# A hybrid conv/retention decoder block: values ahead of the previous head's projection, later norm sums, a regrouped last score block and a shared tail

## The chip, the core and the metric

The kernel runs on one core of one Trainium2 chip. The core has five engines that run side by side and meet only at semaphores: TensorE (PE, with its weight loads shown as PEld), VectorE (DVE), ScalarE (ACT), GpSimd (POOL) and SyncE (SP), which issues most of the DMAs. The metric is the device time of one execution in microseconds; lower is better.

## The reference, cut to what matters

One decoder layer over 512 tokens of width 1024, in float32:

```python
h = rms_norm(x, norm_mix_g)
glu_in, q, k, v, g, gate_logits = split(h @ w_in)
a   = glu_in[:C] * sigmoid(glu_in[C:])             # conv branch
a   = silu(layer_norm(causal_depthwise_conv31(a)))
y_a = a @ w_conv_proj + conv_proj_b
q, k = rotary(q) * dk**-0.5, rotary(k)             # 4 heads, dk 256, dv 512
r   = retention(q, k, v)                           # (q k^T * decay) v, causal
r   = (r - mean(r)) * rsqrt(var(r) + eps)          # per head
y_b = (silu(g) * r * ret_norm_g) @ w_ret_proj
x   = x + (sigmoid(gA) * y_a + sigmoid(gB) * y_b) @ w_out
u   = causal_depthwise_conv3(rms_norm(x, norm_ffn_g) @ w_up)
x   = x + (silu(u[:F]) * u[F:]) @ w_down
out = rms_norm(x, norm_final_g)
```

## The kernel before

Everything is held transposed: features on the 128 partitions, the 512 tokens along the free axis. Each float32 matrix product is made of three passes in the reduced format fp32r, high*high, high*low and low*high, so every activation and every weight is split into a high and a low part (ACT makes the high one, DVE the low one). `unit` makes one 128-feature block of output: for 8 k-tiles, three matmuls of 512 columns each, 24 in all, into one of the 8 PSUM banks. Weights come as one stream of half-megabyte pieces in the order of use (`load_half`, `split_half`: ACT line 130, DVE line 131), two pieces ahead.

The four heads run in a loop. Head h makes four GLU blocks (its two convolution channels' inputs), two blocks of q and two of k with their rotation (`rope`), then, from head 1 on, the projection of head h-1's result (`ret_proj`, 8 units of 12 matmuls), then the values (`values`, 96 matmuls into four banks at once, lines 509 to 511), the scores (`scores`, four key blocks j of 512, 384, 256 and 128 query columns), four gate units, and the product of scores and values (`inner`). The depthwise convolution of 31 taps runs on DVE (line 451) at low priority, between other work. After the heads come the gates, the two output projections, the FFN and the tail.

Norms need a sum over partitions and then a reciprocal root of it on all partitions. `stat` does it in stages that are spread over the units by a counter: `later(n, fn)` runs `fn` when `tick()` has been called n times, and `unit` calls `tick()` once. First DVE folds the squares (lines 275 and 277), then, `wait[0]` ticks later, one matmul sums them (line 281), DVE takes the diagonal out (lines 292 and 297), GpSimd raises it to the power -0.5 (line 245), and two DMAs by way of DRAM spread the row over the partitions into tile `rB` or `nB`; `use` is called `wait[1]` ticks after that. For the first norm the ticks come in `unit_quad`, which runs four GLU blocks together over 8 k-tiles (12 matmuls each): one tick after k-tile `QSUM` = 5, one after the last. For a head's norm the waits are (3, 2), its `use` being lines 603 and 209 on DVE. The convolution's layer norm (`conv_norm`) starts after head 3: at its fourth tick `centre` writes the mean into a tile `muB` (ACT line 467), which takes the slot of tag `nB` (one buffer, shared with the head norm's row), DVE subtracts it (line 470) and sums squares, and four ticks later comes the matmul of line 281 for the variance.

The Tile framework orders the instructions of each engine ahead of time: it simulates the kernel with its own costs and lets each engine take, of the instructions that are ready in that simulation, the one that stands first in the program (with the priorities given). On the chip each engine then runs its list strictly in that order.

The tail works on the two token halves (256 columns). `late_half` makes the last two blocks of the down projection for one half (lines 739 to 741), with callbacks between its matmuls; `finish` gives the stages of the final norm. `early` sums what is known before the last block (four small matmuls, line 229), `first` adds the last block's square (four more) and takes the root on GpSimd, `second` spreads the root over the partitions with four matmuls (line 260, `fB`) and multiplies the eight blocks by it on DVE (line 779), two blocks to a tile, each tile sent out by one DMA from SP (line 781).

Of the kernel before, what the change touches and what calls it, by code (L numbers as in the profile page):

```python
# [14 lines left out]
P = 128  # L15
S = 512
# [13 lines left out]
LOOK = 2  # L30
QSUM = 5
WARM = 9
# [17 lines left out]
def hybrid_block(  # L50
# [29 lines left out]
    def tmp():  # L80
        return t512("t", 8)

    def bank():
        return psp.tile([P, S], F32, tag="ps", name=nm("ps"))
# [11 lines left out]
    warm = sb.tile([P, NCH], F32, tag="tok", bufs=8, name="warm")  # L96
    for tag, bufs, dt in (("x", 8, F32), ("xg", 16, F32R), ("A", 16, F32R), ("C", 8, F32),
                          ("R", 8, F32R), ("G", 4, F32), ("ss", 2, F32), ("t", 8, F32),
                          ("rB", 1, F32), ("nB", 1, F32), ("dec", 1, F32)):
        first[tag] = sb.tile([P, S], dt, tag=tag, bufs=bufs, name=nm(tag))  # L100
    cosr = sb.tile([P, S], F32, tag="cosr", name="cosr")
# [20 lines left out]
    raws = {}  # L122

    def load_half(h):
        raw = wide("wraw", F32, HS, 3)
        nc.sync.dma_start(out=raw, in_=wst[h])
        raws[h] = raw
# [84 lines left out]
    def split_scaled(src, g, tag, bufs):  # L212
        h = t512(tag, bufs, F32R)
        l = t512(tag, bufs, F32R)
# [33 lines left out]
    def spread_ps(ps, r, chunks=range(NCH)):  # L248

        sl = slice(chunks[0], chunks[-1] + 1)  # L250
        rh = tok(F32R)
        rl = tok(F32R)
        nc.vector.tensor_copy(out=rh[:, sl], in_=r[:, sl])
        nc.vector.tensor_tensor(out=rl[:, sl], in0=r[:, sl], in1=f32(rh[:, sl]), op=ALU.subtract)

        def run():
            for c in chunks:
                dst = ps[:, c * P:(c + 1) * P]
                for i, x in enumerate((rh, rl)):
                    nc.tensor.matmul(dst, lhsT=x[:, c:c + 1].broadcast_to([P, P]), rhs=identr,  # L260
                                     start=i == 0, stop=i == 1)
            return ps

        return run
# [197 lines left out]
    def conv_norm():  # L462
        run = sums(csum[0])

        def centre():
            muB = t512("nB", 1)
            nc.scalar.mul(out=muB, in_=run(), mul=1.0 / D)
# [6 lines left out]
        def scale(rs, _):  # L474
            for i in range(KT):
# [3 lines left out]
                                     scale=pcol("conv_ln_g", i), bias=pcol("conv_ln_b", i))  # L479
                h = t512("A", 16, F32R)  # L480
                l = t512("C", 8, F32R)
# [7 lines left out]
    def rope(p1=None):  # L489
# [3 lines left out]
        for u, v, op in ((p1, p2, ALU.subtract), (p2, p1, ALU.add)):  # L493
# [4 lines left out]
            nc.vector.tensor_tensor(out=m1, in0=m1, in1=m2, op=op)  # L498
            res.append(split(m1, "A", 16))
        return res  # L500

    def values():
# [12 lines left out]
        for c in range(NCH):  # L515
# [5 lines left out]
            nc.vector.tensor_scalar(out=m, in0=s, scalar1=-1.0 / DV, scalar2=None, op0=ALU.mult)  # L521
            h = t512("A", 16, F32R)
            l = t512("A", 16, F32R)
            nc.scalar.activation(out=h, in_=t, func=AF.Identity, bias=m)
# [7 lines left out]
    def scores(q, k, dec):  # L532
        sc = wide("sc", F32R, 2 * SW, 1)
        sh, sl_ = sc[:, :SW], sc[:, SW:]
        for j in range(NCH):
# [3 lines left out]
            for d in range(2):  # L539
                (qh, ql), (kh, kl) = q[d], k[d]  # L540
                nc.tensor.matmul(ps[:, :n], lhsT=kh[:, js], rhs=qh[:, j * P:], start=d == 0,
# [5 lines left out]
            t = tmp()  # L547
            nc.vector.tensor_tensor(out=t[:, :n], in0=ps[:, :n], in1=dec[:, :n], op=ALU.mult)
            o = slice(SOFF[j], SOFF[j] + n)
# [43 lines left out]
    def ret_norm(h, banks, sg):  # L593
# [11 lines left out]

        stat(sq.acc, DV, EPS, use, (3, 2), "nB")
        return res
# [15 lines left out]
    for h in range(H):  # L623
# [27 lines left out]
    conv_norm()  # L651
    sigA = [gate(m, t512("A", 16)) for m in range(KT)]
    for mp in range(KT // 2):
# [98 lines left out]
    def finish(half):  # L752
# [7 lines left out]
        def early(sqs):  # L760
# [24 lines left out]
        return early, first, second  # L785

    a_sums, a_rsqrt, a_out = finish(0)
    sqs = late_half(0, {(LATE - 1, HF - 2): a_sums})
    b_sums, b_rsqrt, b_out = finish(1)
    sqs = late_half(1, {(0, 4): lambda _: a_rsqrt(sqs), (1, 1): a_out, (LATE - 1, HF - 2): b_sums})  # L790
    b_rsqrt(sqs)
    b_out(None)
    assert pos[0] == 8 * NBLK
# [102 lines left out]
```

## Time and profile before

| | before |
|---|---|
| median of 3 runs | 1075.55 us (1075.36 to 1075.80) |
| profiled execution, its own time | 1075.43 us |
| span of the profiled execution | 1073.3 us |
| PE busy | 1058.7 us, 99% |
| DVE busy | 780.5 us, 73% |
| ACT busy | 429.7 us, 40% |
| mean granted TensorE clock | 0.996 |

The span runs from the first to the last instruction; 2.1 us of the execution's time lie outside it. A time of an instruction in a timeline is its start from the begin of the span. Matmuls overlap in the pipeline, so their durations are longer than the distance from one start to the next, and that distance is what counts.

### The profile page before, as it was taken

The numbers are of one execution on the slowest core, as the hardware profiler recorded it, in microseconds if no ns is written. First come the engines' busy times: TensorE is split into PE (matmuls) and PEld (weight loads), VectorE is DVE, ScalarE is ACT, GpSimd is POOL, SyncE is SP. The second block draws the span as 40 slices with busy tenths as digits, with TensorE's granted clock in tenths as the row PEclk, the third lists the DMA queues.
The fourth block names the chain that finished last, engine by engine and source line by source line (L and its number), as shares of the span: only waits on it lengthen the run. The fifth ranks groups of instructions, "written<-read, shape, count | busy, mean of one in ns | idle before, by whom it ended". The sixth has DMA issues, their size and how long they took to land.

```text
span 1073.3 us, 12462 instructions
## 1 busy us (share of the span) xinstructions
PE 1058.7 (99%) x4810; PEld 883.5 (82%) x4810; DVE 780.5 (73%) x1173; ACT 429.7 (40%) x577; POOL 26.1 (2%) x88
## 2 busy tenths in 40 slices
PE   9999999999999999999899999999999999999996
PEld 7888788888888888888788888888888888888886
DVE  7799989958997899957765555587776336777433
ACT  6343433543334431544552333354444113444331
POOL 0100100000000000000000000000000000000000
PEclk9999999999999999999999999999999999999999
DMA  8322232223223222223223442233222222222312
GB/s 286 100 97 90 62 105 94 93 80 98 101 95 99 71 96 99 82 78 106 89 99 99 146 128 98 91 105 110 98 98 93 98 93 92 96 99 98 98 59 79
DMA packets 34122, 107.32 MB, mean 100 GB/s; under 512 B 4048, under 2 KB 6992, under 8 KB 34064
## 3 DMA queue, kind: packets, MB, share of 16 engines
q1 hardware_dynamic: 32848, 104.42, 29.4%
q0 software_dynamic: 784, 1.85, 0.7%
q8 instruction: 37, 0.61, 0.2%
q10 hardware_dynamic: 432, 0.27, 0.1%
q14 instruction: 21, 0.17, 0.1%
HBM read 104.41 MB, written 2.11 MB: 99 GB/s over the span
## 4 chain that ended last, share of the span: by engine, by line
PE 84%; DVE 10%; DMA 2%; issue 2%; ACT 1%; POOL 0%; SPq 0%; POOLq 0%; DVEq 0%
PE ps L179 25%; PE ps L181 25%; PE ps L180 25%; DVE C L451 3%; PE ps L510 2%; PE ps L511 2%; PE ps L509 2%; DVE wlo L131 2%; PE ps L572 1%; DVE ss L221 1%; PE ps L574 1%; DMA G<-in_wst_dram 1%; DVE t L421 0%; DMA nB<-row 0%; DMA rB<-row 0%
## 5 line engine op out<-in xcount | busy, mean ns | idle before, releaser
L130 ACT CAST whi<-wraw 128x1024 fp32r<-128x1024 f32 (+2 forms) x184 | 191.5, 1041 | 319.6 <-PE ps L180 214.5
L131 DVE TENSOR_TENSOR wlo<-wraw,whi 128x1024 fp32r<-128x1024 f32 (+2 forms) x185 | 222.5, 1203 | 62.4 <-ACT whi L130 61.0
L181 PE MATMUL ps<-xg,wlo 128*128 128x512 f32 x656 | 256.0, 390 | 0.0
L179 PE MATMUL ps<-xg,whi 128*128 128x512 f32 x656 | 256.0, 390 | 0.0
L180 PE MATMUL ps<-xg,whi 128*128 128x512 f32 x656 | 256.0, 390 | 0.0
L181 PE MATMUL ps<-A,wlo 128*128 128x512 f32 x448 | 174.3, 389 | 0.0
L179 PE MATMUL ps<-A,whi 128*128 128x512 f32 x448 | 174.3, 389 | 0.0
L451 DVE SCALAR_TENSOR_TENSOR C<-ap,par,C 128x512 f32<-128x512 f32 x240 | 166.8, 740 | 2.3 <-ACT C L448 1.9
L180 PE MATMUL ps<-A,whi 128*128 128x512 f32 x384 | 149.4, 389 | 0.0
L181 PEld LDWEIGHTS ps<-xg,wlo 128*128 128x128 f32 x656 | 123.5, 188 | 25.8
L180 PEld LDWEIGHTS ps<-xg,whi 128*128 128x128 f32 x656 | 123.5, 188 | 25.6
L179 PEld LDWEIGHTS ps<-xg,whi 128*128 128x128 f32 x656 | 123.6, 188 | 25.3
L181 PEld LDWEIGHTS ps<-A,wlo 128*128 128x128 f32 x448 | 84.1, 188 | 17.5
L179 PEld LDWEIGHTS ps<-A,whi 128*128 128x128 f32 x448 | 84.1, 188 | 17.5
L180 PEld LDWEIGHTS ps<-A,whi 128*128 128x128 f32 x384 | 72.1, 188 | 14.9
L693 DVE SCALAR_TENSOR_TENSOR t<-ap,par,t 128x512 f32<-128x512 f32 x96 | 71.4, 748 | 1.7 <-issue 0.2
L221 DVE TENSOR_TENSOR x<-x,ps 128x512 f32<-128x512 f32 (+1 forms) x50 | 33.1, 661 | 52.6 <-PE ps L181 49.1
L687 DVE TENSOR_TENSOR ap<-ps,rB 128x512 f32<-128x512 f32 x48 | 32.8, 687 | 40.9 <-PE ps L181 37.7
L179 PE MATMUL ps<-R,whi 128*128 128x512 f32 x160 | 62.2, 389 | 0.0
L180 PE MATMUL ps<-R,whi 128*128 128x512 f32 x160 | 62.2, 389 | 0.0
L181 PE MATMUL ps<-R,wlo 128*128 128x512 f32 x160 | 62.2, 389 | 0.0
L421 DVE TENSOR_TENSOR t<-ps,rB 128x512 f32<-128x512 f32 x48 | 32.5, 684 | 33.9 <-PE ps L181 33.8
(154 smaller groups left out, 1204.8 us busy)
## 6 DMA issues: line engine op xcount, KB each, us to landing
wraw<-in_wst_dram SPq DMA_DIRECT2D x180, 512.0 KB, 3.3
x<-in_xT_dram SPq DMA_DIRECT2D x16, 256.0 KB, 3.3
out_dram<-t SPq DMA_DIRECT2D x8, 256.0 KB, 2.1
nB<-row POOLq DMA_DIRECT2D x5, 256.0 KB, 4.5
dec<-in_decay_dram SPq DMA_DIRECT2D x4, 256.0 KB, 2.6
wraw<-in_wst_dram SPq DMA_DIRECT2D x3, 256.0 KB, 5.3
G<-in_wst_dram SPq DMA_DIRECT2D x2, 256.0 KB, 5.7
t<-in_cs_dram SPq DMA_DIRECT2D x2, 256.0 KB, 3.9
```

Source lines behind the costliest of these rows:

```text
L130: (eng or nc.scalar.copy)(out=hi[:, sl], in_=raw[:, sl])
L131: nc.vector.tensor_tensor(out=lo[:, sl], in0=raw[:, sl], in1=f32(hi[:, sl]), op=ALU.subtract)
L179: nc.tensor.matmul(ps, lhsT=wh, rhs=xh, start=kt == 0, stop=False)
L180: nc.tensor.matmul(ps, lhsT=wh, rhs=xl, start=False, stop=False)
L181: nc.tensor.matmul(ps, lhsT=wl, rhs=xh, start=False, stop=kt == last)
L221: nc.vector.tensor_tensor(out=acc, in0=acc, in1=v, op=ALU.add)
L421: nc.vector.tensor_tensor(out=t, in0=ps, in1=rB[0], op=ALU.mult)
L451: nc.vector.scalar_tensor_tensor(out=acc, in0=a[:, k:k + S], scalar=wcol(k), in1=acc, op0=ALU.mult, op1=ALU.add)
L509: nc.tensor.matmul(banks[c], lhsT=xh[:, sl], rhs=wh, start=kt == 0, stop=False)
L510: nc.tensor.matmul(banks[c], lhsT=xl[:, sl], rhs=wh, start=False, stop=False)
L687: nc.vector.tensor_tensor(out=u[:, FK - 1:], in0=ps, in1=rB[0], op=ALU.mult)
L693: nc.vector.scalar_tensor_tensor(out=c, in0=u[:, k:k + S], scalar=wcol(k), in1=c, op0=ALU.mult, op1=ALU.add)
```

## The change

Five edits. Head h's values come before head h-1's projection, and the loads follow that order (`use_order`). The ticks of the norms move: `QSUM` from 5 to 6, the heads' waits from (3, 2) to (4, 3), and `muB` takes the slot of tag `dec` in place of `nB`. Of the score block j = 3 (128 query columns), the two products that share the weights `kh` become one matmul over 256 columns, high and low part of q side by side; ACT copies and DVE adds the two halves of the result afterwards. For that the high and the low part of a split lie in one tile of tag `A` (8 tiles of 1024 columns in place of 16 of 512). In the tail, half 0 makes its sum once (`whole`) in place of `early` and `first`, its callbacks come one k-tile later, and of half 1 the products of blocks 6 and 7 go to GpSimd, from a copy of the root that ACT takes out of a second spread, and out by a DMA from ACT; six matmuls whose results nobody reads are put between the tail's steps (`idle_work`).

```diff
-QSUM = 5
+QSUM = 6
...
+    def pair_a():
+
+        t = wide("A", F32R, 2 * S, 8)
+        return t[:, :S], t[:, S:], t.rearrange("p (i t) -> p i t", i=2)
...
+    use_order = list(range(NBLK))
+    for h in range(1, H):
+        b = 20 * h + 4
+        use_order[b:b + 8] = use_order[b + 4:b + 8] + use_order[b:b + 4]
+
     def load_half(h):
         raw = wide("wraw", F32, HS, 3)
-        nc.sync.dma_start(out=raw, in_=wst[h])
+        nc.sync.dma_start(out=raw, in_=wst[use_order[h]])
...
         def centre():
-            muB = t512("nB", 1)
+            muB = t512("dec", 1)
...
-                (qh, ql), (kh, kl) = q[d], k[d]
+                (qh, ql, qb), (kh, kl, _) = q[d], k[d]
+                if j == NCH - 1:
+                    for low in ((False, True) if d == 0 else (True, False)):
+                        if low:
+                            nc.tensor.matmul(ps[:, :n], lhsT=kl[:, js], rhs=qh[:, j * P:],
+                                             start=False, stop=False)
+                        else:
+                            nc.tensor.matmul(ps[:, :2 * n].rearrange("p (i t) -> p i t", i=2),
+                                             lhsT=kh[:, js], rhs=qb[:, :, j * P:],
+                                             start=d == 0, stop=d == 1)
+                    continue
...
+            if j == NCH - 1:
+                src = tmp()
+                nc.scalar.copy(out=src[:, :n], in_=ps[:, n:2 * n])
+                nc.vector.tensor_tensor(out=src[:, :n], in0=ps[:, :n], in1=src[:, :n], op=ALU.add)
+            nc.vector.tensor_tensor(out=t[:, :n], in0=src[:, :n], in1=dec[:, :n], op=ALU.mult)
...
-        stat(sq.acc, DV, EPS, use, (3, 2), "nB")
+        stat(sq.acc, DV, EPS, use, (4, 3), "nB")
...
         k = rope()
+        v = values()
         if rg is not None:
             ret_proj(h - 1, rg)
-        v = values()
...
+        def whole(sqs):
+            for q in sqs:
+                add_into(ss.acc[:, tk], q[:, :HT])
+            tok_sums(ps, [(ss.acc, 0)], chunks)
+            run.append(spread_ps(ps, rsqrt(scaled(ps, D, EPS, sl), sl), chunks))
...
         def second(_):
-            fB = run[0]()
-            for m in range(0, KT, 2):
+            fB = run[0]()[:, tk]
+            if half:
+                fS = tmp()[:, :HT]
+                nc.scalar.copy(out=fS, in_=run[0](bank())[:, tk])
+            for m in (KT - 2, *range(0, KT - 2, 2)) if half else range(0, KT, 2):
                 o = tmp()
+                aside = half and m == KT - 2
+                eng = nc.gpsimd if aside else nc.vector
                 for i in range(2):
-                    nc.vector.tensor_tensor(out=o[:, i * HT:(i + 1) * HT], in0=fB[:, tk],
-                                            in1=x1[m + i][:, tk], op=ALU.mult)
-                nc.sync.dma_start(
+                    eng.tensor_tensor(out=o[:, i * HT:(i + 1) * HT], in0=fS if aside else fB,
+                                      in1=x1[m + i][:, tk], op=ALU.mult)
+                (nc.scalar if aside else nc.sync).dma_start(
...
+    def idle_work(ps, n):
+
+        for _ in range(n):
+            nc.tensor.matmul(ps, lhsT=onesr, rhs=ff[HF][0], start=True, stop=True)
+
+    _, _, a_rsqrt, a_out = finish(0)
+    sqs = late_half(0, {})
+    b_sums, b_rsqrt, _, b_out = finish(1)
+    sqs = late_half(1, {(0, 5): lambda _: a_rsqrt(sqs), (1, 2): a_out, (LATE - 1, HF - 2): b_sums})
+    spare = bank()
+    idle_work(spare, 2)
     b_rsqrt(sqs)
+    idle_work(spare, 4)
     b_out(None)
```

## Rows read from the trace of the kernel before

**Rows 1.** Waits: engine, line, releaser; us in total, times, longest us.
```profile
PE ps L281 <- DVE t L277: 5.5, 3, 3.2
...
PE ps L260 <- DVE tokr L253: 1.2, 1, 1.2
...
PE ps L229 <- ACT t L747: 1.0, 1, 1.0
```
**Rows 2.** Timeline of PE: start us, us, what, [idle before].
```profile
23.60 0.61 PE L196 MATMUL ps<-xg,R 128*128 128x512 f32 x2
24.77 0.47 PE L281 MATMUL ps<-t,onesr 128*128 128x512 f32 x1 [0.56 <-DVE t L277]
...
121.17 0.39 PE L181 MATMUL ps<-xg,wlo 128*128 128x512 f32 x1
123.34 0.47 PE L281 MATMUL ps<-t,onesr 128*128 128x512 f32 x1 [1.78 <-DVE t L277]
...
511.23 0.39 PE L181 MATMUL ps<-xg,wlo 128*128 128x512 f32 x1
514.82 0.50 PE L281 MATMUL ps<-t,onesr 128*128 128x512 f32 x1 [3.20 <-DVE t L277]
...
518.77 0.42 PE L179 MATMUL ps<-xg,whi 128*128 128x512 f32 x1
```
**Rows 3.** Windows: stretch, its us, busy us of each engine, PEclk, DMA share, GB/s.
```profile
36.00:121.00 85.00, 85.00 (x396) 71.49 (x395) 84.97 (x135) 33.84 (x50) 0.24 (x2) 1.00 0.26 84
...
515.00:519.00 4.00, 4.00 (x11) 3.16 (x12) 3.96 (x10) 2.98 (x5) 0.00 (x0) 0.57 0.13 39
...
1069.00:1072.00 3.00, 0.00 (x0) 0.00 (x0) 1.22 (x4) 0.00 (x0) 0.00 (x0) 0.50 0.99 350
```
**Rows 4.** Timelines of DVE and ACT from 487 to 515 us.
```profile
487.00 0.17 DVE L297 TENSOR_SCALAR tok<-tok 128x4 f32<-128x4 f32 x1
...
495.29 1.90 DVE L603 TENSOR_TENSOR G<-G,nB 128x512 f32<-128x512 f32 x3 [3.49 <-DMA nB<-row]
...
498.42 0.60 ACT L467 ACTIVATE nB<-ps 128x512 f32<-128x512 f32 x1 [0.23 <-DVE G L603]
...
500.05 2.49 DVE L470 TENSOR_TENSOR C<-C,nB 128x512 f32<-128x512 f32 x4
...
514.08 0.69 DVE L277 TENSOR_TENSOR t<-t,t 64x512 fp32r<-64x512 f32 x1
```
**Rows 5.** DVE's instructions by line from 500 to 514.8 us; count, busy us, mean ns.
```profile
L209 DVE TENSOR_TENSOR R<-G,R 128x512 fp32r<-128x512 f32 x2 | 1.4, 676 | 0.0
```
**Rows 6.** Timeline of PE at head 0's last score block.
```profile
75.25 0.28 PE L545 MATMUL ps<-A,A 128*128 128x256 f32 x1
75.37 0.22 PE L541 MATMUL ps<-A,A 128*128 128x128 f32 x1
...
76.27 0.39 PE L180 MATMUL ps<-xg,whi 128*128 128x512 f32 x1
76.50 0.39 PE L181 MATMUL ps<-xg,wlo 128*128 128x512 f32 x1
```
**Rows 7.** Timelines of PE and DVE in the tail.
```profile
1052.86 0.28 PE L741 MATMUL ps<-xg,wlo 128*128 128x256 f32 x1
...
1053.55 0.28 PE L740 MATMUL ps<-xg,whi 128*128 128x256 f32 x1
...
1067.48 2.74 DVE L779 TENSOR_TENSOR t<-ps,x 128x256 f32<-128x256 f32 x8 [0.64 <-PE ps L260]
```
**Rows 8.** Timeline of POOL, its two copies of 128 columns.
```profile
1.08 0.29 POOL L390 CAST onesr<-ones 128x128 fp32r<-128x128 f32 x1
...
16.42 0.61 POOL L389 CAST identr<-ident 128x128 fp32r<-128x128 f32 x1 [15.05 <-DMA ident<-in_ident_dram]
```
**Rows 9.** Timeline of DVE in head 1.
```profile
130.35 0.68 DVE L421 TENSOR_TENSOR t<-ps,rB 128x512 f32<-128x512 f32 x1
...
137.60 1.89 DVE L603 TENSOR_TENSOR G<-G,nB 128x512 f32<-128x512 f32 x3 [4.18 <-DMA nB<-row]
```

More of the change, by code (lines that the diff above doesn't have):

```diff
@@ L81, in tmp, with half_a @@
         return t512("t", 8)
+    spare = {}
+    def pair_a():
+        t = wide("A", F32R, 2 * S, 8)
+        return t[:, :S], t[:, S:], t.rearrange("p (i t) -> p i t", i=2)
+    def half_a(dt=F32R):
+        if dt not in spare:
+            t = wide("A", dt, 2 * S, 8)
+            spare[dt] = t[:, S:]
+            return t[:, :S]
+        return spare.pop(dt)
     def bank():
@@ L96, in hybrid_block @@
     warm = sb.tile([P, NCH], F32, tag="tok", bufs=8, name="warm")
-    for tag, bufs, dt in (("x", 8, F32), ("xg", 16, F32R), ("A", 16, F32R), ("C", 8, F32),
+    for tag, bufs, dt in (("x", 8, F32), ("xg", 16, F32R), ("A", 8, F32R), ("C", 8, F32),
                           ("R", 8, F32R), ("G", 4, F32), ("ss", 2, F32), ("t", 8, F32),
                           ("rB", 1, F32), ("nB", 1, F32), ("dec", 1, F32)):
-        first[tag] = sb.tile([P, S], dt, tag=tag, bufs=bufs, name=nm(tag))
+        w = 2 * S if tag == "A" else S
+        first[tag] = sb.tile([P, w], dt, tag=tag, bufs=bufs, name=nm(tag))
     cosr = sb.tile([P, S], F32, tag="cosr", name="cosr")
@@ L212, in split_scaled @@
     def split_scaled(src, g, tag, bufs):
-        h = t512(tag, bufs, F32R)
-        l = t512(tag, bufs, F32R)
+        if tag == "A":
+            h, l, _ = pair_a()
+        else:
+            h = t512(tag, bufs, F32R)
+            l = t512(tag, bufs, F32R)
         nc.scalar.activation(out=h, in_=src, func=AF.Copy, scale=g)
@@ L254, in spread_ps, with run @@
         nc.vector.tensor_tensor(out=rl[:, sl], in0=r[:, sl], in1=f32(rh[:, sl]), op=ALU.subtract)
-        def run():
+        def run(dst=ps):
             for c in chunks:
-                dst = ps[:, c * P:(c + 1) * P]
                 for i, x in enumerate((rh, rl)):
-                    nc.tensor.matmul(dst, lhsT=x[:, c:c + 1].broadcast_to([P, P]), rhs=identr,
-                                     start=i == 0, stop=i == 1)
-            return ps
+                    nc.tensor.matmul(dst[:, c * P:(c + 1) * P], rhs=identr, start=i == 0,
+                                     lhsT=x[:, c:c + 1].broadcast_to([P, P]), stop=i == 1)
+            return dst
         return run
@@ L479, in scale @@
                                      scale=pcol("conv_ln_g", i), bias=pcol("conv_ln_b", i))
-                h = t512("A", 16, F32R)
+                h = half_a()
                 l = t512("C", 8, F32R)
@@ L498, in rope @@
             nc.vector.tensor_tensor(out=m1, in0=m1, in1=m2, op=op)
-            res.append(split(m1, "A", 16))
+            h, l, both = pair_a()
+            nc.scalar.copy(out=h, in_=m1)
+            nc.vector.tensor_tensor(out=l, in0=m1, in1=f32(h), op=ALU.subtract)
+            res.append((h, l, both))
         return res
@@ L521, in values @@
             nc.vector.tensor_scalar(out=m, in0=s, scalar1=-1.0 / DV, scalar2=None, op0=ALU.mult)
-            h = t512("A", 16, F32R)
-            l = t512("A", 16, F32R)
+            h, l, _ = pair_a()
             nc.scalar.activation(out=h, in_=t, func=AF.Identity, bias=m)
@@ L539, in scores @@
             for d in range(2):
-                (qh, ql), (kh, kl) = q[d], k[d]
+                (qh, ql, qb), (kh, kl, _) = q[d], k[d]
[4 more added lines that the diff above has]
+                                             start=False, stop=False)
+                        else:
+                            nc.tensor.matmul(ps[:, :2 * n].rearrange("p (i t) -> p i t", i=2),
+                                             lhsT=kh[:, js], rhs=qb[:, :, j * P:],
+                                             start=d == 0, stop=d == 1)
+                    continue
                 nc.tensor.matmul(ps[:, :n], lhsT=kh[:, js], rhs=qh[:, j * P:], start=d == 0,
@@ L547, in scores @@
             t = tmp()
-            nc.vector.tensor_tensor(out=t[:, :n], in0=ps[:, :n], in1=dec[:, :n], op=ALU.mult)
+            src = ps
+            if j == NCH - 1:
[3 more added lines that the diff above has]
+            nc.vector.tensor_tensor(out=t[:, :n], in0=src[:, :n], in1=dec[:, :n], op=ALU.mult)
             o = slice(SOFF[j], SOFF[j] + n)
@@ L651, in hybrid_block @@
     conv_norm()
-    sigA = [gate(m, t512("A", 16)) for m in range(KT)]
+    sigA = [gate(m, half_a(F32)) for m in range(KT)]
     for mp in range(KT // 2):
@@ L774, in second @@
         def second(_):
-            fB = run[0]()
-            for m in range(0, KT, 2):
+            fB = run[0]()[:, tk]
[3 more added lines that the diff above has]
+            for m in (KT - 2, *range(0, KT - 2, 2)) if half else range(0, KT, 2):
                 o = tmp()
+                aside = half and m == KT - 2
+                eng = nc.gpsimd if aside else nc.vector
                 for i in range(2):
-                    nc.vector.tensor_tensor(out=o[:, i * HT:(i + 1) * HT], in0=fB[:, tk],
-                                            in1=x1[m + i][:, tk], op=ALU.mult)
-                nc.sync.dma_start(
+                    eng.tensor_tensor(out=o[:, i * HT:(i + 1) * HT], in0=fS if aside else fB,
+                                      in1=x1[m + i][:, tk], op=ALU.mult)
+                (nc.scalar if aside else nc.sync).dma_start(
                     out=out[m * P:(m + 2) * P, tk].rearrange("(i p) t -> p i t", p=P),
                     in_=o.rearrange("p (i t) -> p i t", i=2))
[L785 to L790, printed above, removed]
+        return early, first, whole, second
+    def idle_work(ps, n):
[7 more added lines that the diff above has]
+    idle_work(spare, 2)
     b_rsqrt(sqs)
+    idle_work(spare, 4)
     b_out(None)
```

## The prediction

> **What bounds the kernel now.** I read the page first. PE is busy 99% of the span, DVE, the next, 73% (the table above), and for nearly the whole span PE starts one 512-column matmul every 0.227 us (0.23 in the two decimals of [rows 6], 76.27 to 76.50). So a time is saved in only two ways: less PE work, or fewer moments in which PE waits. A full list of PE's waits is short, which is why the next view is the one by waits [rows 1]: the matmul of line 281, the partition sum of a norm, waited for DVE 5.5 us in three places, the spread of the root (line 260) 1.2 us once, the tail's sum (line 229) 1.0 us once. Then the timeline of PE at those three places [rows 2] gives each its price as the distance between starts, less the 0.227 that it would be anyhow:
>
> - first norm: two matmuls from 23.60, so the next was due at 24.05; it started at 24.77: **0.72 us**.
> - head 0's norm: 121.17 to 123.34, less 0.227: **1.94 us**.
> - the convolution's layer norm: 511.23 to 514.82, less 0.227: 3.36 us. After it the clock is not whole: over 515 to 519 us the granted clock was 0.57 of 2.4 GHz [rows 3], so mostly at its lower level, 1.2 GHz. From 514.82 to 518.77 PE started ten matmuls in 3.95 us where 2.27 would do: 1.68 us more. Together **5.04 us**. The 1.94 us wait of head 0 was followed by no such loss.
>
> The last stretch is another regime. From 1069 to 1072 us the 16 DMA engines were busy 0.99 of the time and moved 350 GB/s, 1.05 MB, which is just the second half of the output (four tiles of 256 KB) [rows 3]. There the transfer sets the end, not DVE.
>
> **The change part by part.** Each sum is against the profiled execution, 1075.43 us (its span of 1073.3 and 2.1 outside it); the median of the runs is 0.12 higher.
>
> *QSUM 6.* The matmul of line 281 comes one k-tile later: 12 x 0.227 = 2.72 us, by when its input is long there. The 0.72 goes. In exchange the root arrives 2.72 - 0.72 = 2.0 us later, and with it everything that DVE does with it in head 0. PE does not need it at once: the banks that hold unscaled products are given back by DVE, and in the kernel before PE ran on over this whole stretch without a wait. Cost nothing on PE; DVE is 2.0 us later, which the next part must carry.
>
> *Head waits (4, 3).* Line 281 comes after the fourth unit, not the third: 24 x 0.227 = 5.45 us later. At head 0, where PE was due at 121.40, it is due at 126.85, less 0.95 because QSUM and the score block (below) bring PE there earlier: 125.9. DVE: it was busy 84.97 of the 85 us from 36 to 121 [rows 3], so nothing absorbs the later root, and its line 277 that let PE go at 123.34 comes at up to 123.34 + 2.0 + 0.3 (one more short addition for the score block; a 512-column operation is 1.90 / 3 = 0.63 [rows 4], a quarter of the columns at most half of that) = 125.6. It fits by 0.3 us. The planner may put one weight split more before it (1024 columns, so about 2 x 0.63 = 1.3 us): 1.0 us would remain. But the filler on DVE there is the low-priority convolution, which gives way, so I take 0 and keep 0 to 1.0. The 1.94 goes.
>
> *muB in `dec`.* Head 3's norm and the layer norm share the slot `nB`. ACT could write the mean only when line 603 had read the row (498.42, released by L603), DVE began line 470 at 500.05, and line 277 ended at 514.77, 14.7 us later, when PE had stood for 3.4 us [rows 4]. DVE itself waited 3.49 us for the row's DMA before line 603, with line 470 behind it in the order. With `dec`, which is free after head 3's scores, the mean needs only its own sum, four units of 24 before the matmul of 511.46 (due), so at 511.46 - 21.8 = 489.7. Head 3's own sum now stands in the same tick and just before it; its picking on DVE (four operations of 128 columns, at most half of 0.63 each, and line 297's 0.17) takes 1.4, a weight split 1.3: line 470 at about 492.5, line 277 done at 492.5 + 14.7 = 507.2, 4.3 us before PE asks. What could eat that: lines 603 and 209 of head 3 now fall in between, eight operations x 0.63 = 5.0 us, of which the 14.7 already hold two [rows 5], so 3.8; and the planner believes in the row sooner than it comes, so DVE can stand before line 603 again, up to the 3.49 of before. Worst: 507.2 + 3.8 + 3.5 = 514.5, a wait of 3.0 us. All three have lower rank in the program than the layer norm's chain, so they get only its gaps. I take 0, keep 0 to 3.0. The 5.04 goes, and the clock's 1.68 with it.
>
> *Values ahead of the projection.* The same matmuls and loads in another order; the swap is made in `use_order` too, and SP passes as many bytes. The head norm's row, 5.45 us later by its wait, is wanted 96 x 0.227 = 21.8 us later. Scores come after the projection, so the values' eviction on ACT has more time than before. Nothing; what it could cost is the rival that ends on the other side.
>
> *Score block j = 3.* Six 128-column matmuls: 75.37 to 76.27 less the one unit matmul's 0.227 = 0.67 us, 0.11 each though 256 columns take only 0.12 (75.25 to 75.37) [rows 6]: a matmul of 128 columns pays for its weights, not for its columns. Now two of 256 and two of 128: at 0.12 and 0.11 each 0.46, saving 0.21 to (if a short one next to a long one hides its weights) 0.27 a head. The strided pair of q could run slower than a plain 256; the bound there is no gain at all. I take 0.22 x 4 = **0.9 us**, keep 0 to 1.1. ACT's copy and DVE's addition lie under the four gate units (21.8 us) between scores and `inner`.
>
> *Pairs in `A`.* As many bytes in the same order of use: nothing; a pair's slot comes free with the later of its halves, and both were read by the same unit.
>
> *Tail, sums.* Half 0's separate early sum goes: 1052.86 to 1053.55 holds two matmuls of 256 (0.24) and the four small ones [rows 7]: 0.69 - 0.24 = **0.45 us** of PE. The callbacks one k-tile later give DVE time for its two additions.
>
> *Tail, products.* By DVE alone the last tile would be ready two products earlier, 2 x 2.74 / 8 = 0.69 us [rows 7]. But the transfer is the limit [rows 3]: it starts when the first tile is there, which is no earlier, and four tiles still have to pass. So I take 0. The Trainium skill says the same of the second queue (DMA: Bandwidth & Descriptors, Issuing engines are not separate DMA queues: DMAs started by different engines run on the same 16 DMA engines); before, no DMA was issued from ACT in the tail, so no row shows it, and without that rule the sum would be 0.69 lower. GpSimd may be late: the nearest rows are copies of 128 columns at 0.29 and 0.61 [rows 8], so 256 columns 0.58 to 1.22, two 1.2 to 2.4 us. They start about 1.05 us after DVE's first product (a second spread, four matmuls x 0.11, and ACT's copy, at most the 0.60 of its 512 columns in [rows 4]), so end 2.2 to 3.5 after it. The transfer starts 1069 - 1067.48 = 1.5 after that product, 0.8 after the first tile; three tiles take three quarters of 3 us, to 3.75, so the fourth must be ready by 2.95. Late by 0 to 0.55. The Trainium skill is against such work (GPSIMD Engine Reference, Elementwise — side-by-side cycle accounting: a two-input addition took 1.96 times VectorE's time); by it two products would take 2 x 2 x 0.34 = 1.4 us, which is inside the bounds and would leave the sum as it is.
>
> *Idle matmuls.* Two (0.45) in PE's wait of 1.0, four (0.91) in its wait of 1.2 [rows 1]: nothing; without that cover at most 0.3.
>
> Sum: 0.72 + 1.94 + 5.04 + 0.9 + 0.45 = 9.05. 1075.43 - 9.05 = 1066.38, so **1066.4 us**.
>
> **The rivals.**
>
> - *One wait comes back in part.* DVE is late at head 0 (0 to 1.0), at the layer norm (0 to 3.0), or GpSimd at the end (0 to 0.55): up to 4.6, 1067.4 to 1071.0. For it: DVE saturated to 121, the planner's optimism in all heads. Against: the margin of 4.3 us at the layer norm.
> - *The layer norm's wait stays whole,* because the planner puts line 603 before line 470 after all: 5.04 back, 1071.4 us. For it: that is today's order. Against: it was forced by the shared slot.
> - *Slower: values find no banks.* `values` needs four banks at once, right behind `rope`; the projection needed one every 2.7 us. Today DVE evicts the fourth GLU block at 130.35 and stands 4.18 us before line 603 at 137.60 [rows 9]; with the later wait that stop moves to about 143, in front of q's and k's rotations. If it also stood before a GLU eviction, more than four of eight banks were held when values start (150.9) and PE waited. It decides against the change from 9.05 / 3 = 3.0 us a head on; a wait like the layer norm's (3.36 + 1.68) in three heads gives 1066.4 + 15.1 = 1081.5. Against: the evictions lie 20 us before, and head 0 already runs in this order, without a wait.
> - *The change does not do it:* the waits move behind one another (DVE's work is the same), within 2 us of before.
>
> **How the numbers follow.** Likeliest (1065.4 to 1067.4): 0.6. One wait in part: 0.23. Layer norm's wait whole: 0.08. No change: 0.05. Slower: 0.04. The range goes down by the score block's best case (0.2) and by a transfer that gains the 0.69 after all, to 1065.4; and up to the end of the second case, 1071.0; it leaves out 0.17. A measurement here tells about 0.2%, 2.15 us, from nothing: faster 0.91, same 0.05, slower 0.04.
>
> **What would show it.** Line 281 without idle time before it near 26.8, 126 and 511 (less the shift), and a granted clock of 1.00 throughout; line 470 before or between lines 603, eight us earlier; 0.45 us for the four matmuls of block 3; one group of four line-229 matmuls less; DMA share 0.99 for 3 us at the end as before, with DVE's last product 0.7 us earlier relative to its first. Wrong, if PE shows a wait at line 509 in heads 1 to 3, a wait of over 2 us at line 281, or an end that comes after GpSimd's tile.

## The result and the profile after

The changed kernel took 1067.01 us (median of 6 runs, 1066.19 to 1067.72), the kernel before, beside it on the same chip, 1075.45 us (6 runs, 1073.30 to 1075.84): a ratio of 0.9925, 95% interval 0.9912 to 0.9938. Timed again later it took 1066.71 us (5 runs), ratio 0.9919 (0.9904 to 0.9933). The profiled execution of the changed kernel took 1067.37 us with a span of 1065.4 us and a mean granted clock of 0.998.

The changed code lies some 20 to 50 lines further down: the unit's matmuls 179 to 181 are now 200 to 202, line 196 of the quad is 217, the norm's sum 281 is 304, DVE's folds 275 and 277 are 298 and 300, the mean's copy 467 and subtraction 470 are 490 and 493, the head norm's product 603 is 643, the spread 260 is 283 and the output products 779 are 830.

The head of the page, its busy shares and the chain that ended last:

```profile
span 1065.4 us, 12477 instructions
...
PE 1056.8 (99%) x4808; PEld 882.5 (83%) x4808; DVE 780.3 (73%) x1175; ACT 429.6 (40%) x582; POOL 28.1 (3%) x90
...
PE 98%; DMA 0%; issue 0%; POOL 0%; ACT 0%; SPq 0%; POOLq 0%; DVE 0%
```

PE's busy time is 1.9 us less, the span 7.95 us: most of what was won is time in which PE had stood (14.6 us before, 8.6 after). PE's waits over the whole span (engine, line, releaser; us in total, times, longest), against [rows 1]:

```profile
PE ps L217 <- ACT R L151: 1.0, 1, 1.0
PE ps L345 <- POOL neghalf L341: 1.0, 1, 1.0
PE ps L283 <- DVE tokr L277: 0.9, 1, 0.9
```

None is at a norm's sum, where there were three waits, 5.5 us together. What is left is one wait in the start (line 217), one before the first useful matmul and one in the tail. The tail's other wait, 1.0 us before line 229 (now 253), is not won: idle matmuls fill it. PE's timeline at the three places of [rows 2]:

```profile
25.53 0.61 PE L217 MATMUL ps<-xg,R 128*128 128x512 f32 x2
25.98 0.39 PE L304 MATMUL ps<-t,onesr 128*128 128x512 f32 x1
...
126.64 0.39 PE L202 MATMUL ps<-xg,wlo 128*128 128x512 f32 x1
126.86 0.39 PE L304 MATMUL ps<-t,onesr 128*128 128x512 f32 x1
...
508.61 0.39 PE L202 MATMUL ps<-xg,wlo 128*128 128x512 f32 x1
508.84 0.39 PE L304 MATMUL ps<-t,onesr 128*128 128x512 f32 x1
509.06 0.39 PE L200 MATMUL ps<-xg,whi 128*128 128x512 f32 x1
```

Each sum follows the matmul before it by the usual 0.22 to 0.23 us. Three windows that answer to [rows 3] (busy us of PE, PEld, DVE, ACT, POOL; then the granted clock, the DMA share and GB/s):

```profile
36.00:121.00 85.00, 85.00 (x395) 71.44 (x394) 83.75 (x133) 33.27 (x50) 0.12 (x1) 1.00 0.26 85
508.00:512.00 4.00, 4.00 (x19) 3.31 (x18) 4.00 (x7) 3.33 (x6) 0.00 (x0) 1.00 0.32 116
...
1061.00:1064.00 3.00, 0.00 (x0) 0.00 (x0) 0.38 (x2) 0.00 (x0) 0.60 (x1) 0.50 0.99 348
```

Around the layer norm's sum the granted clock is 1.00 (2.4 GHz) where it was 0.57, and the last transfer runs as before. The chain in front of that sum, on ACT and DVE, against [rows 4]:

```profile
487.60 0.59 ACT L490 ACTIVATE dec<-ps 128x512 f32<-128x512 f32 x1
...
489.08 0.69 DVE L493 TENSOR_TENSOR C<-C,dec 128x512 f32<-128x512 f32 x1
...
499.29 0.69 DVE L643 TENSOR_TENSOR G<-G,nB 128x512 f32<-128x512 f32 x1 [0.23 <-DMA nB<-row]
...
504.76 0.69 DVE L300 TENSOR_TENSOR t<-t,t 64x512 fp32r<-64x512 f32 x1
```

The mean is written 10.8 us earlier (2.6 of them because PE as a whole is ahead by that much), DVE subtracts it ahead of line 643 instead of behind it, and the fold is done at 505.45, 3.4 us before PE asks at 508.84. At head 0 the same fold ended at 125.06, 1.8 us before PE asked at 126.86.

For a reckoning, the span is cut at three marks of PE: the first unit matmul behind the opening quad, the first matmul of `late_half`, and its last one.

| us | before | after | difference |
|---|---|---|---|
| start to end of the quad | 28.71 | 28.93 | +0.22 |
| quad to `late_half` (heads to FFN) | 1016.00 | 1008.04 | -7.96 |
| `late_half`, first to last matmul | 18.91 | 18.47 | -0.44 |
| last matmul to the end | 9.69 | 9.92 | +0.23 |
| span | 1073.31 | 1065.36 | -7.95 |

### The profile page after: what moved, and what is told of

The parts are those of the page before. It is cut to its first block, busy times and chain, and to the rows that moved or that the text cites. A ratio compares the mean times of both kernels' runs of the same rounds, so it can differ in the third digit from the quotient of the medians.

```text
span 1065.4 us, 12477 instructions
## 1 busy us (share of the span) xinstructions
PE 1056.8 (99%) x4808; PEld 882.5 (83%) x4808; DVE 780.3 (73%) x1175; ACT 429.6 (40%) x582; POOL 28.1 (3%) x90
## 4 chain that ended last, share of the span: by engine, by line
PE 98%; DMA 0%; issue 0%; POOL 0%; ACT 0%; SPq 0%; POOLq 0%; DVE 0%
PE ps L202 27%; PE ps L201 27%; PE ps L200 27%; PE ps L537 3%; PE ps L536 3%; PE ps L535 3%; PE ps L217 2%; PE ps L612 2%; PE ps L614 1%; PE ps L779 1%; PE ps L780 1%; PE ps L781 1%; DMA x<-in_xT_dram 0%; PE ps L580 0%; PE ps L576 0%; PE ps L578 0%
```

## The experiments

Each was compared with the kernel before on the same chip. "Body" is the distance from the end of the quad to the end of the span in the profile, 1044.60 us before and 1036.43 after; it leaves out the start, which varies (last section).

**One edit alone on the kernel before.** First the mean's slot:

```diff
-            muB = t512("nB", 1)
+            muB = t512("dec", 1)
```

> The kernel before with muB in the slot of tag dec alone. My theory: the shared slot is the whole cause of the wait before the layer norm's matmul (3.36 us and 1.68 of lost clock), so about 5.0 us faster, 1070.4, with the waits at the first norm (0.72) and at head 0 (1.94) as before. Rival: the later ticks (4, 3) give the margin and the slot alone gives less than 2 us.

1070.60 us, ratio 0.9946 (0.9929 to 0.9963). Its sum at 512.10 follows without idle time and the clock behind it is whole; in the list of waits one at such a line is left, head 0's:

```profile
512.00:516.00 4.00, 4.00 (x20) 3.30 (x19) 3.96 (x11) 3.13 (x5) 0.00 (x0) 1.00 0.08 13
```
```profile
PE ps L281 <- DVE t L277: 1.5, 1, 1.5
```

The body is 5.44 us shorter: the layer norm's 5.04 and a little of head 0's wait. So the slot alone makes more than half of the change's gain. The wait at the first norm, expected as before, was 0.1 us this time. Second the later waits:

```diff
-        stat(sq.acc, DV, EPS, use, (3, 2), "nB")
+        stat(sq.acc, DV, EPS, use, (4, 3), "nB")
```

> The kernel before with the head norms' waits (4, 3) alone. My theory: the 1.94 us at head 0 go, but without the swap the projection's inputs (line 209) come after PE asks for them, up to 5 us in each of three heads, and the row in nB is read one unit later, so the layer norm's wait of 3.4 grows by up to 5.4: slower in sum, 1079 to 1092. Rival: the projection is fed in time and the layer norm's wait is the same, 1.9 us faster, 1073.5.

1092.56 us, ratio 1.0152 (1.0135 to 1.0169), just beyond the expectation. PE's waits:

```profile
PE ps L281 <- DVE t L277: 9.1, 2, 8.3
PE ps L180 <- DVE R L209: 4.9, 8, 1.2
PE ps L179 <- ACT R L208: 1.6, 3, 0.5
```

and the windows about the layer norm's sum, which started at 531.38 behind a matmul of 522.64:

```profile
515.00:531.00 16.00, 8.03 (x36) 6.32 (x34) 15.84 (x24) 9.72 (x16) 0.00 (x0) 0.83 0.28 97
531.00:536.00 5.00, 4.62 (x11) 3.65 (x12) 4.00 (x14) 2.98 (x5) 0.78 (x1) 0.51 0.02 7
```

Head 0's wait is gone, as the edit means; the shorter of the two at line 281 is the first norm's:

```profile
25.47 0.47 PE L281 MATMUL ps<-t,onesr 128*128 128x512 f32 x1 [0.79 <-DVE t L277]
```

But the later root meets two consumers: in the old order the projection, which stands right behind `rope` and waits for the operands of lines 208 and 209 in heads 1 to 3, and the mean, still behind the row in slot `nB`. Behind the layer norm's wait the clock is low (0.51 in the second window, so nearly all at 1.2 GHz); behind the projection's waits it fell in head 1 alone (0.83 over 145 to 158 us, against 1.00 over 276 to 284 and 400 to 406). The edit alone loses 17 us. Third `QSUM`:

```diff
-QSUM = 5
+QSUM = 6
```

> The kernel before with QSUM 6 alone. My theory: the 0.7 us before the first norm's matmul go and DVE, full from 36 to 121 us, gets the root 2.0 us later; with the head waits still (3, 2) its line 277 comes after PE asks, so head 0's wait of 1.94 grows to between 1.9 and 4.6: within 0.7 us faster and 2 us slower, 1075 to 1077.5. Rival: the planner moves low-priority convolution away, head 0's wait stays under 1.0 or goes, 1074 or less.

1078.12 us, ratio 1.0026 (1.0016 to 1.0037), slightly beyond the expectation. The first norm's wait is gone, and head 0's has grown, on PE's timeline:

```profile
121.26 0.39 PE L181 MATMUL ps<-xg,wlo 128*128 128x512 f32 x1
125.00 0.76 PE L281 MATMUL ps<-t,onesr 128*128 128x512 f32 x1 [3.35 <-DVE t L277]
125.56 0.63 PE L179 MATMUL ps<-xg,whi 128*128 128x512 f32 x1
```

125.00 - 121.26 - 0.23 = 3.51 us, against 1.94. Behind it the granted clock was low:

```profile
125.00:129.00 4.00, 4.00 (x11) 3.18 (x12) 3.93 (x13) 2.63 (x4) 0.00 (x0) 0.61 0.28 100
```

That loss (eleven matmuls where there is room for 17.6, so 1.5 us) was in no expectation. DVE is so full up to there that most of the root's delay goes through to head 0's fold; what `QSUM` 6 wins, it loses later unless the waits are (4, 3).

**One edit taken out of the changed kernel.** The order of values and projection, in the loads and in the loop:

```diff
-        use_order[b:b + 8] = use_order[b + 4:b + 8] + use_order[b:b + 4]
+        use_order[b:b + 8] = use_order[b:b + 4] + use_order[b + 4:b + 8]
...
-        v = values()
         if rg is not None:
             ret_proj(h - 1, rg)
+        v = values()
```

> The changed kernel with the values behind the projection again, loads too. My theory: the swap costs nothing itself and pays for the later waits; in the changed kernel's trace the last split of head 0's result ends at 155.7 while the projection would ask from 148.9 on, so some 4 to 5 us of wait in each of three heads, 1079 to 1083. Rival: the planner ranks these splits higher when they are wanted sooner, no wait, 1067.

1077.83 us, ratio to before 1.0017 (1.0007 to 1.0028), a smaller loss than was expected; the body is 1047.35, 10.9 us longer than the changed kernel's. PE's waits and the first of those places:

```profile
PE ps L201 <- DVE R L230: 4.6, 7, 1.8
PE ps L200 <- ACT R L229: 2.0, 3, 1.0
```
```profile
150.00:156.00 6.00, 3.97 (x10) 2.61 (x11) 6.00 (x9) 2.08 (x4) 0.00 (x0) 0.76 0.26 87
```

6.6 us of waits, all at the projection's operands, and in head 1 the low clock behind them. So without the swap, which was costed at nothing, the whole gain is lost: it gives the later root the 21.8 us of the values to arrive in. Since the kernel before had no waits in heads 1 to 3, what the later waits and the swap buy together is head 0's wait alone (1.94 us); this follows from the lists of waits, no run has the change without both. Then the mean's slot:

```diff
-            muB = t512("dec", 1)
+            muB = t512("nB", 1)
```

> The changed kernel with muB in nB again. My theory: the mean cannot be written before line 643 has read the row, which comes one unit later than in the kernel before, so the layer norm's matmul waits 3.4 to 8.8 us and the clock falls: 5 to 10.5 us slower than the changed kernel, 1072 to 1077.5. Rival: (4, 3) moves enough work away that less than 2 us of wait come back.

1076.44 us, ratio to before 1.0007 (0.9997 to 1.0017). One wait has come, and the lower level of the clock with it:

```profile
PE ps L304 <- DVE t L300: 7.8, 1, 7.8
```
```profile
516.00:520.00 4.00, 3.61 (x9) 2.84 (x10) 3.86 (x14) 2.99 (x5) 0.00 (x0) 0.50 0.04 16
```

The wait is longer than the 3.36 us of before, because with (4, 3) the row that the slot waits for comes later. Then the score block, with the branches for j = 3 off, and the idle matmuls:

```diff
-                if j == NCH - 1:
+                if False:
...
-            if j == NCH - 1:
+            if False:
```

> The changed kernel with six matmuls of 128 columns for the last score block, as before. My theory: per head the block and the matmul behind it take 0.20 to 0.22 us more, 0.8 in all, and no wait appears elsewhere. Rival: the two wide matmuls with their strided operand take as long, difference under 0.1 a head.

1067.38 us in its one run; from the quad to `late_half` 1008.81, 0.77 us more than in the changed kernel.

```diff
-    spare = bank()
-    idle_work(spare, 2)
     b_rsqrt(sqs)
-    idle_work(spare, 4)
     b_out(None)
```

> The changed kernel without the six idle matmuls. My theory: nothing moves: from the last matmul of line 781's kind to the first of the spread 3.08 us as in both kernels, granted clock in the spread 1.00. Rival: without them the clock falls before the spread, whose eight matmuls then take 0.1 us more each.

1066.20 us in its one run; all stretches of the table but the start agree with the changed kernel within 0.01 us, and the clock over the spread of the root was 1.00:

```profile
1057.50:1058.40 0.90, 0.87 (x7) 0.86 (x8) 0.25 (x2) 0.00 (x0) 0.00 (x0) 1.00 0.00 0
```

In this execution the idle matmuls would have hidden nothing.

**The tail.** All products back on DVE, no second spread, no copy, DMAs from SP:

```diff
-            if half:
-                fS = tmp()[:, :HT]
-                nc.scalar.copy(out=fS, in_=run[0](bank())[:, tk])
-            for m in (KT - 2, *range(0, KT - 2, 2)) if half else range(0, KT, 2):
+            for m in range(0, KT, 2):
                 o = tmp()
-                aside = half and m == KT - 2
+                aside = False
...
-                    eng.tensor_tensor(out=o[:, i * HT:(i + 1) * HT], in0=fS if aside else fB,
+                    eng.tensor_tensor(out=o[:, i * HT:(i + 1) * HT], in0=fB,
```

> The changed kernel with all eight last products on DVE and all DMAs from SP, without the second spread, ACT's copy and GpSimd's products; the idle matmuls stay. My theory: the transfer of 1 MB is the limit, and the last tile, from GpSimd, is late for it: from DVE's first product to the end 5.8 us as in the kernel before, not 6.1 as in the changed one, so 0.2 to 0.3 faster, which only the trace can show. Rival: the sharing helps, and it is over 0.3 us slower.

1066.85 us, ratio 0.9925 (0.9910 to 0.9941): in the medians it is the changed kernel. In the profile the last stretch is 9.69 again, 0.23 us shorter than with the shared products. To find where the 0.23 lies, and whether the tail can be made shorter, three more kernels ran, and the changed kernel once more as their control.

> The changed kernel itself, unaltered, timed again beside the next run. If its times differ from run to run only by the start (when the first x tiles land), every execution lies in 1066.0 to 1068.0 us, the median near 1067.0, and the distance from the last matmul of the first quad to the end of the span is that of the first profile (1065.4 - 28.9 = 1036.4 us) within 0.2, whatever the start was. If instead the body varies, that distance moves with the time.

1066.71 us (1066.44 to 1067.56); body 1036.44, the start 0.75 us shorter than in the first profile and the span 0.74. The first theory holds: the two profiles agree to 0.01 us in everything but the start.

The next kernel has DVE make all products, as the first kernel of this part did, leaves the idle matmuls out and splits the first tile of half 1:

```diff
+                    if half and m == 0:
+                        (nc.scalar if i else nc.sync).dma_start(
+                            out=out[(m + i) * P:(m + i + 1) * P, tk], in_=o[:, i * HT:(i + 1) * HT])
+                if half and m == 0:
+                    continue
...
-    spare = bank()
-    idle_work(spare, 2)
     b_rsqrt(sqs)
-    idle_work(spare, 4)
```

> The changed kernel with the tail's products all on VectorE again, without the copy, the second spread and the idle matmuls, and with the first pair of half 1 sent as two DMAs of one block each (one from SP, one from ACT), so that the transfer can begin one product (0.33 us) earlier. Theory A (the output transfer of 1 MB sets the end and starts with the first tile): first product to end of span 5.83 - 0.33 = 5.5 us, against 6.06 with the shared products, so 0.5 us less, about 1066.5 us. Theory B (the fixed time of a DMA from issue to landing sets the end, or smaller DMAs move slower): 5.8 or more, about 1066.8 us. In medians the two lie within the spread of the start, so the distance in the profile decides.

1067.13 us, ratio 0.9920 (0.9908 to 0.9933); 6.24 us from the first product to the end. Theory A is refuted: the last landing stayed at 4.92 us though the first DMA was issued 0.33 us earlier. B's "5.8 or more" holds, but 6.24 is more than a fixed landing explains. Two things had gone wrong. The spread itself was slow; the windows of this kernel, and below them PE's row of the spread:

```profile
1057.00:1058.00 1.00, 0.00 (x0) 0.00 (x0) 0.19 (x2) 0.00 (x0) 0.70 (x1) 1.00 0.00 0
1058.00:1059.50 1.50, 1.11 (x4) 0.93 (x4) 0.45 (x3) 0.00 (x0) 0.00 (x0) 0.56 0.00 0
```
```profile
1058.17 1.11 PE L283 MATMUL ps<-identr,tokr 128*128 128x128 f32 x4 [1.23 <-DVE tokr L277]
```

Without the idle matmuls PE stood twice, 0.96 and 1.23 us, and the clock fell to its lower level under the spread: 1.16 us from the spread's start to the first product, against 0.78 in the changed kernel. The run without idle matmuls above had the same waits and a clock of 1.00 there. Of six profiles without idle matmuls (the kernel before and its three variants among them) this one alone shows the low clock at the spread, of eight with them none; so they may hide a loss of 0.4 us that comes in some executions, which one case does not prove. And behind the last landing there was more to do. At the end of the kernel SP waits for its semaphores of DMAs one after another; their events in the traces (us from the start of DVE's first product of half 1):

| kernel | last landing seen | waits after it | end |
|---|---|---|---|
| before | 4.94 | 0 | 5.83 |
| changed | 4.99 | 3 | 6.06 |
| all products on DVE | 4.95 | 0 | 5.83 |
| the same, half 1's first tile split, no idle matmuls | 4.92 | 7 | 6.24 |
| all on DVE, half 0's first tile split | 4.94 | 7 | 6.27 |
| all on DVE, every block its own DMA | 4.61 | 0 | 5.50 |

(The last two kernels follow below.) Each wait takes 0.06 to 0.07 us even if its semaphore has long been set. To test that the order of these waits costs time, one DMA more was put in, in half 0, beside the idle matmuls and with all products on DVE. Half 0's two small DMAs were issued 6.8 and 6.4 us before half 1's first product and had landed 4.6 us before it:

```diff
+                    if half == 0 and m == 0:
+                        (nc.scalar if half and i else nc.sync).dma_start(
+                            out=out[(m + i) * P:(m + i + 1) * P, tk], in_=o[:, i * HT:(i + 1) * HT])
+                if half == 0 and m == 0:
+                    continue
...
```

> As the run with all products on VectorE and four tiles for half 1, only that the first tile of half 0 is sent as two DMAs, 8 us before the end, so that there are nine output DMAs and not eight. Theory A (at the end SP waits for the eight DMA semaphores one after another in a fixed order, 0.07 us each, and the ninth DMA has the one that is looked at first): the last landing stays 4.95 us behind the first product, but seven more waits follow it, so first product to end is 5.83 + 0.4 = 6.25 us. Theory B (the order of the waits costs nothing, and the longer end of the shared tail comes from the transfer alone): 5.83 us.

1069.23 us in its one run, whose quad ended at 30.81, the latest start of all. The last landing was seen at 4.94, and the end came at 6.27: the first theory's 6.25. SP waited for the last DMA's semaphore first, and the seven settled ones followed.

Last, every block by its own DMA, 16 of them, so that the last is also the last to be looked at:

```diff
                 for i in range(2):
...
+                    nc.vector.tensor_tensor(out=o[:, i * HT:(i + 1) * HT], in0=fB,
+                                            in1=x1[m + i][:, tk], op=ALU.mult)
+                    if True:
+                        (nc.scalar if half and i else nc.sync).dma_start(
+                            out=out[(m + i) * P:(m + i + 1) * P, tk], in_=o[:, i * HT:(i + 1) * HT])
+                continue
...
```

> The changed kernel with the tail's products all on VectorE, the idle matmuls kept, no copy and no second spread, and every 128x256 block sent as its own DMA (half 1 from SP and ACT in turn), 16 output DMAs in all. Theory A (the last landing is set by VectorE's pace plus the time of the last DMA: last product 2.75 us after the first, plus 1.7 us that a 128 KB DMA took from issue to landing): the last DMA lands 4.45 us after the first product's start, against 4.92 to 4.99 in four arrangements so far; it is also the last that SP's closing waits look at, so the span ends 0.9 us behind it: first product to end 5.35 us, against 6.06 in the changed kernel, 0.7 us less, about 1066.3 us. Theory B (the transfer of 1 MB takes its 3 us plus fixed times whatever the tiles): landing at 4.9, end at 5.8, about 1066.8 us.

1066.53 us (5 runs, 1065.83 to 1067.07), ratio 0.9920 (0.9907 to 0.9934). The landing came at 4.61 and the end at 5.50, 0.56 us less than in the changed kernel (expected 5.35); body 1035.88. DVE's products and the output DMAs (KB each, median us from issue to landing):

```profile
1059.79 2.74 DVE L825 TENSOR_TENSOR t<-ps,x 128x256 f32<-128x256 f32 x8 [0.64 <-PE ps L283]
```
```profile
out_dram<-t SPq DMA_DIRECT2D x4, 128.0 KB, 1.8
out_dram<-t ACTq DMA_DIRECT2D x4, 128.0 KB, 1.8
```

DVE's 2.74 and the last DMA's 1.8 give 4.54, close to the 4.61. It is the shortest body of all the kernels; its median lies 0.2 to 0.5 us below the changed kernel's two, which the spread of the runs doesn't separate.

## Why the prediction was right, and where its sizes were off

The forecast was 1066.4, in a range of 1065.4 to 1071.0; 1067.01 was measured. From the quad to `late_half`, where the head 0, layer norm and score terms lie, the sum gave 1.94 + 5.04 + 0.9 = 7.88 us; 7.96 was measured. The profiled execution is 1.0 us longer than its forecast: 0.94 of that lies in the start and 0.23 in the tail, and small differences give 0.2 back. By its own terms (0.2 and 0.69) the range would begin at 1065.5; nothing hangs on it. The pairs in `A` had no run of their own; no wait came with them.

- *QSUM 6 and the first norm's wait.* The wait is gone in all eleven profiles with `QSUM` 6. But 0.72 us was one execution's price: the two other profiles with 5 had 0.1 and 0.79 us of idle time there. The profiled pair shows none of the gain, since ACT read the second x tile 1.1 us later (last section), and the start is 0.22 longer in place of 0.72 shorter. Where that tile was read when it had been before (5.84 us), the quad ended earlier than at 28.71, at 28.40 in the kernel with the old score block and at 28.16 in the one without the swap:

```profile
5.82 0.72 ACT L239 ACTIVATE xg<-x,g 128x512 fp32r<-128x512 f32 x1 [0.91 <-DMA x<-in_xT_dram]
```
```profile
5.85 0.72 ACT L239 ACTIVATE xg<-x,g 128x512 fp32r<-128x512 f32 x1 [0.99 <-DMA x<-in_xT_dram]
```

  So some of the 0.72 seems to be there, 0.31 and 0.55 us in these two; how much in general is not settled. The half sentence "DVE is 2.0 us later, which the next part must carry" is what the run with `QSUM` alone shows: 1.6 us more at head 0, and a loss of clock.
- *Head waits (4, 3).* Margin of 0.3 us forecast, 1.8 measured in the first profile and 2.1 in the second; of the bound of 1.0 nothing came. DVE was busy 83.75 us from 36 to 121, not 84.97, so it did find some slack; why the fold came before the 125.6 that was worked out is not shown. The edit alone loses 17 us, which the prediction didn't work out.
- *muB in `dec`.* Line 470 (now 493) was due at about 492.5, 19.0 us before the sum's matmul at 511.46, and began at 489.08, 19.8 us before it (508.84): DVE did the split and the first subtraction between the pickings. From there to the end of the fold it took 16.4 us, not 14.7, so the fold came 3.4 us before PE asked, against 4.3. The bound for DVE's stand before the row (up to 3.49) was nearly free: 0.23.
- *The swap.* "Nothing" was right as a sum, given the waits, but it was this edit that paid for (4, 3): 10.9 us without it. PE did not wait at the values' matmuls; the rival of the missing banks did not come, though DVE still stood before the row in head 1, as foreseen:

```profile
143.73 0.69 DVE L643 TENSOR_TENSOR G<-G,nB 128x512 f32<-128x512 f32 x1 [3.29 <-DMA nB<-row]
```

- *Score block.* 0.77 us, 0.19 a head, against 0.22. PE's timeline at head 0's last block, to be read against [rows 6]:

```profile
75.59 0.28 PE L572 MATMUL ps<-A,A 128*128 128x256 f32 x1
75.70 0.34 PE L569 MATMUL ps<-A,A 128*128 128x128 f32 x2
75.88 0.33 PE L572 MATMUL ps<-A,A 128*128 128x256 f32 x1
76.05 0.40 PE L200 MATMUL ps<-xg,whi 128*128 128x512 f32 x1
```

76.05 - 75.59 = 0.46, the very sum of two at 0.12 and two at 0.11; the strided pair costs no more than plain columns.
- *Tail sums.* 0.44 against 0.45.
- *Tail products.* This term was mis-sized: 0 forecast, 0.23 us lost. In the changed kernel the transfer held the end, as said: 0.99 of the DMA engines in both, at 350 GB/s before and 348 after, and the last landing seen 4.94 and 4.99 us behind the first product. GpSimd was not late: its tile was ready at 1061.61, 2.31 us behind the first product, within the 2.95. It was the last to land, which the prediction named among its signs of being wrong, but its DMA was issued at 2.33, 0.44 us before the last DMA of the kernel before (2.77), and landed no earlier (4.97 against 4.93): it stood behind the other tiles.

```profile
1059.30 2.08 DVE L830 TENSOR_TENSOR t<-ps,x 128x256 f32<-128x256 f32 x6 [0.64 <-PE ps L283]
```
```profile
1060.20 1.41 POOL L830 TENSOR_TENSOR t<-t,x 128x256 f32<-128x256 f32 x2 [1.93 <-ACT t L824]
```

Of the 0.23, 0.05 is the later landing. The rest, 0.18, is three closing waits on SP: the ACT DMA, the last to land, has the fourth semaphore from the end, so three settled ones are looked at after it. Both rules of the Trainium skill agree with the trace. Issuing engines are not separate DMA queues (DMA: Bandwidth & Descriptors), since the DMAs of all of them run on the same 16 DMA engines: with one DMA from ACT no more was moved in a second, 348 against 350 GB/s. Elementwise — side-by-side cycle accounting (GPSIMD Engine Reference) has an addition on GpSimd at 1.96 times VectorE's time: 0.70 us for a product on GpSimd and 0.34 to 0.35 on DVE is 2.0 times. That "the transfer sets the end, not DVE" is half of it: in the old tail two limits met at 4.93. The transfer needed 4.15 us from its first issue at 0.78, and the last tile, issued at 2.77 by DVE's pace, needed 2.16 to land. Relieving one is not enough: with GpSimd's share the last issue came earlier and the end stayed; with the first tile split the first issue came at 0.45, and the end stayed. With single blocks the first issue comes at 0.45 and the last piece needs only 1.82, and the landing comes 0.33 earlier.
- *Idle matmuls.* They cost nothing: 3.08 us from the last matmul of `late_half` to the spread with them and without. Five ran in the first wait and one in the second, not two and four:

```profile
1055.56 1.31 PE L841 MATMUL ps<-C,onesr 128*128 128x512 f32 x5
```

  Without them nothing was lost in one execution and 0.4 in another; the bound given was 0.3.

## What to carry to other kernels

Edits that delay a result to spare a wait can be worth less than nothing one by one: two of these lost 3 and 17 us alone, and paid only because another edit gave the later result something to arrive under; follow a delayed value to its next consumer before costing it. A shared single-buffer slot can put a short chain behind a long round trip, and moving it to a slot that is free by then won 5 us here at no cost. Where a tail is one transfer, look at four things apart: when its first piece is issued, when its last one is, how small that last piece is, and what is still looked at after it has landed.

## What the runs showed of the hardware that was not expected

- Waits on settled semaphores are not free: 0.06 to 0.07 us each on SP, so the order of the closing waits against the order of landing moved the end by up to 0.44 us.
- The clock falls behind some stalls and not others. PE stood 1.9 us at head 0 and kept 2.4 GHz; behind 3.4 us in the same place the next 4 us had 0.61. With the same two short waits in the tail (0.96 and 1.23 us), one profile shows 1.00 over the spread and another 0.56. What decides it these runs don't show.
- The start varies by more than most of these terms. In eleven profiles with `QSUM` 6 the quad ended at 27.94 to 30.81 us, in three with 5 at 28.71 to 29.68. ACT's second tile, before and after:

```profile
5.84 0.72 ACT L215 ACTIVATE xg<-x,g 128x512 fp32r<-128x512 f32 x1 [0.85 <-DMA x<-in_xT_dram]
```
```profile
6.94 0.72 ACT L239 ACTIVATE xg<-x,g 128x512 fp32r<-128x512 f32 x1 [1.92 <-DMA x<-in_xT_dram]
```

It waits for the second x tile. In the changed kernel's second profile it started at 6.14, 0.80 us earlier, and the quad ended 0.75 us earlier. Why that DMA lands when it does was not tried. The latest start, 30.81, has a second cause: after a wait of 1.35 us at line 217 its clock was low. Two kernels that read the tile as late (7.41 and 7.42, against its 7.36) had no such stretch and ended the quad at 29.41 and 29.42.

```profile
8.50:12.00 3.50, 3.50 (x9) 2.73 (x10) 3.50 (x9) 3.50 (x9) 0.00 (x0) 0.51 0.93 255
```
